# Wider value projections and a split pool of raw weight buffers in a PE-bound mLSTM / HGRN2 trunk

## The chip, the cores and the metric

The kernel runs on one core of one Trainium2 chip. The metric is device time in microseconds (us) of one execution; a version is judged by the median of several. TensorE (PE) multiplies matrices: a stationary operand of 128 x 128 is loaded first (PEld), then a moving operand of up to 512 columns streams through, and results accumulate in PSUM, eight banks of 512 float32 columns per partition. VectorE (DVE) and ScalarE (ACT) do elementwise work, GpSimd (POOL) a little, and SyncE (SP) issues nearly all transfers from memory, in the order of its queue.

## The reference

One layer over 512 tokens of width 1024, in float32. One projection `u = x W_in + b_in` of 14,344 columns feeds two mixers:

- A, mLSTM, four heads of width 512: query and key (causal convolution of four taps, SiLU), value, output gate, and two scalar gates per head. `h = num / max(|den|, exp(-m))`, where `num` is the decayed, causal score matrix times the values and `den` its row sum; then a LayerNorm per head and a sigmoid gate.
- B, HGRN2, eight heads of width 128: forget gate f, key 1 - f, query (SiLU), value ("input" `hi`), output gate; a gated recurrence, a root-mean-square norm and a sigmoid gate.

Then

```
mix = (sigmoid(g_A) * (h_A P_A) + sigmoid(g_B) * (h_B P_B)) W_out
x = LN(alpha x + mix)
x = LN(alpha x + (silu(x W_gate) * (x W_up)) W_down)
```

The kernel computes both recurrences in closed form over the 512 tokens: for mLSTM a 512 x 512 causal weight matrix per head, for HGRN2 a chain of block levels per pair of heads.

## The kernel before, in words

**Float32 products.** Every large product is made from two float32r parts of each operand, `hi` (a rounded copy, ACT) and `lo` (the rest, DVE), as three matmuls: hi hi, hi lo, lo hi (`mm3`, L83 to L86). `split` (L88) makes the two parts.

**Weights.** `fetch` loads a chunk of weights of 512 KB into a raw buffer (`load_w`, L91: pool `rp`, tag `wraw`, five buffers, `WRAW`) and splits it (`split_w`, L96: three buffers each of `whi` and `wlo`). A raw buffer is free again when both halves of the split have read it. A chunk is 24 matmuls of 512 columns, or 48 of 256.

**Two forms of projection.** `proj_sub` (L141) makes 128 features of all 512 tokens: the weights are stationary, x transposed (`xh`, `xl`) moves with 512 columns. `natural_proj` (L156) makes 256 features with tokens on the partitions: x is stationary, the weights move with 256 columns; four row tiles of 128 tokens share two PSUM banks of pool `pp`, and `natural_half` (L149) adds four of the eight k steps from one chunk.

**The stages, in the order of the code.**

1. x is loaded and transposed. The first 256 value columns of head 0 and the scalar gates are projected from a separate load, 264 columns at a time.
2. Four mLSTM heads (loop at L455): eight chunks of key and query features with the score matmuls, the projection onto P_A of the head before (`project_a`), the values (`natural_proj` and `values`, L474 to L477: two calls per head, one for head 0), four chunks of the output gate, with attention (`attend`, L397) and transposes in between. The value tiles `vh`, `vl` have 514 columns: 256 values, two columns of ones (which give `den`), 256 values. Attention makes two products, of 258 and 256 columns.
3. Two chunks of the first merge gate, and the last `project_a`. Then the pool `mp` of the mLSTM stage is closed and the pool `hp` of the HGRN2 stage takes its memory.
4. Four pairs of HGRN2 heads (`h_units`, L527): f, query, values (`natural_proj`, two adds of 512 columns into `v`), output gate: eight chunks per pair. The block levels of a pair (`h_chain`, L711) run while the next pair is projected.
5. Fourteen more chunks of merge gates; `sgb`, in the buffers of f, K, Q and v, keeps the gates of B.
6. Projection onto P_B (L738), eight chunks: DVE multiplies with the gate, adds the A side, and the sum is split into `mxh`, `mxl`.
7. The pools `hp` and `pp` are closed (L744 to L746). Pool `lp` (L750) opens on the side of `rp`, and takes memory that `hp` had: `lng`, `lnb` (LayerNorm rows, L756 and L757), `z` (rows of x, L827), and small tiles. `natural_pass` (L774) multiplies with W_out, two row tiles at a time, in eight chunks of one k step by 1024 columns, each chunk adding to what the first began. LayerNorm, the gate and up projections and the down projection (22 chunks, twice) follow.

**What sets the order.** `defer(n, f)` puts work off until n ticks have passed, and each projected chunk ends with a `tick`: so the small matmuls of attention and of the chain are written between chunks. The tile framework then plans the order on each engine and queue: work that is ready goes first, and among ready work what stands first in the code. It adds the waits. A tile waits for its buffer, and a pool that is opened on memory of a closed pool waits for it.

Of the kernel before, what the change touches and what calls it, by code (L numbers as in the profile page):

```python
# [8 lines left out]
F32 = mybir.dt.float32  # L9
# [20 lines left out]
O_HQ, O_HF, O_HI, O_HG, O_GA, O_GB = 8200, 9224, 10248, 11272, 12296, 13320  # L30
SOFF = [0, 512, 896, 1152]
SCOLS = 1280
WRAW = 5


@with_exitstack
def tile_hybrid_trunk(
# [50 lines left out]
    def split(src, hi, lo):  # L88
        return nc.scalar.copy(hi, src), nc.vector.tensor_sub(lo, src, hi.bitcast(F32))  # L89

    def load_w(src, kk, nn):  # L91
        raw = rp.tile([P, kk, nn], F32, tag="wraw", name="wraw", bufs=WRAW)
        nc.sync.dma_start(raw, src.rearrange("(k p) n -> p k n", p=P))
        return raw

# [7 lines left out]
    def fetch(src, kk, nn):  # L103
        return split_w(load_w(src, kk, nn))
# [4 lines left out]
    def psum(pl, tag, shape=(P, 512), bufs=None):  # L109
        kw = {} if bufs is None else {"bufs": bufs}  # L110
        return pl.tile(list(shape), F32, tag=tag, name=tag, **kw)
# [20 lines left out]
    def tick(w=1.0):  # L132
        for e in pend:
            e[0] -= w
        due = [e for e in pend if e[0] <= 0]
        for e in due:
            pend.remove(e)
        for e in due:
            e[1]()
# [6 lines left out]
                k == 0, k == kk - 1)  # L146
        return ps

    def natural_half(outs, s_, wh, wl, shared=True):  # L149
        for t in range(NT):  # L150
            for k in range(4):
                kx = 4 * s_ + k
                mm3(outs[t], xh[:, kx, t * P:(t + 1) * P], xl[:, kx, t * P:(t + 1) * P], wh[:, k], wl[:, k],
                    kx == 0 and not (shared and t % 2), kx == KD - 1, skip_group_check=True)

    def natural_proj(off):  # L156
        vps = [psum(pp, "pp", (P, 2, 256)) for _ in range(2)]
        outs = [vps[t // 2][:, t % 2] for t in range(NT)]
        for s_ in range(2):
            natural_half(outs, s_, *fetch(win[s_ * 512:(s_ + 1) * 512, off:off + 256], 4, 256))  # L160
            if s_ == 0:
                tick()
        return vps

# [54 lines left out]
        wv.append((hi, lo))  # L219
    vps0 = [psum(*((pp, "pp") if t < 3 else (px, "px")), (P, 264)) for t in range(NT)]  # L220
    for s_ in range(2):
        natural_half(vps0, s_, *wv[s_], shared=False)


    cols = cst.tile([P, 3 * P], F32, name="cols")
# [150 lines left out]
                                           op0=OP.mult, op1=OP.mult)  # L376
            split(w32[:, :n], wth[:, o:o + n], wtl[:, o:o + n])

    def values(h, u2, vps, vt_):
        vh, vl, vb = vt_  # L380
        us2 = slice(u2 * 256, (u2 + 1) * 256)
        vs2 = slice(u2 * 258, u2 * 258 + 256)
        for g in range(2):
            vt = mp.tile([P, 2, 256], F32, tag="w32", name="vt", bufs=4)
            nc.vector.tensor_add(vt, vps[g], vb[:, None, us2].to_broadcast([P, 2, 256]))
            split(vt, vh[:, 2 * g:2 * g + 2, vs2], vl[:, 2 * g:2 * g + 2, vs2])

    def value_tiles(h):
        vh = mp.tile([P, NT, 514], FR, tag="vh", name="vh")
        vl = mp.tile([P, NT, 514], FR, tag="vl", name="vl")  # L390
        nc.vector.memset(vh[:, :, 256:258].bitcast(F32), 1.0)
        nc.vector.memset(vl[:, :, 256:258].bitcast(F32), 0.0)
        vb = mp.tile([P, MD], F32, tag="vb", name="vb")
        nc.sync.dma_start(vb, b_in[:, O_MV + h * MD:O_MV + (h + 1) * MD].to_broadcast([P, MD]))
        return vh, vl, vb

    def attend(h, tiles, wth, wtl, vh, vl, hn):  # L397
        for i in tiles:
            nps = [psum(px, "px", (P, 258)), psum(sp, f"s{i % 3}", (P, 256))]
            for e, vs in enumerate((slice(0, 258), slice(258, 514))):  # L400
                for j in range(i + 1):
                    o = SOFF[j] + (i - j) * P
                    mm3(nps[e], wth[:, o:o + P], wtl[:, o:o + P], vh[:, j, vs], vl[:, j, vs], j == 0, j == i)
            den = nps[0][:, 256:257]
            sm = mp.tile([P, 24], F32, tag="sm", name="sm", bufs=2)
            for e in range(2):
                nc.vector.bn_stats(sm[:, 6 * e:6 * e + 6], nps[e][:, 0:256])
            nc.vector.tensor_scalar(sm[:, 14:15], den, -1.0, em[:, i, h:h + 1], op0=OP.mult, op1=OP.max)
            nc.vector.tensor_tensor(sm[:, 15:16], den, sm[:, 14:15], op=OP.max)
            nc.vector.bn_aggr(sm[:, 12:14], sm[:, 0:12].rearrange("p (a b) -> p a b", a=2))  # L410
            nc.vector.reciprocal(sm[:, 16:17], sm[:, 15:16])
            nc.vector.tensor_mul(sm[:, 17:18], sm[:, 16:17], sm[:, 16:17])
            nc.vector.tensor_scalar(sm[:, 18:19], sm[:, 13:14], sm[:, 17:18], HEAD_EPS, op0=OP.mult, op1=OP.add)
            nc.gpsimd.tensor_tensor(sm[:, 19:20], sm[:, 18:19], nhalf[:, 0:1], op=OP.pow)
            nc.vector.tensor_mul(sm[:, 20:21], sm[:, 19:20], sm[:, 16:17])
            nc.vector.scalar_tensor_tensor(sm[:, 21:22], sm[:, 12:13], -1.0, sm[:, 20:21], op0=OP.mult, op1=OP.mult)
            for e in range(2):
                nc.scalar.activation(hn[:, i, e * 256:(e + 1) * 256], nps[e][:, 0:256], AF.Identity,
                                     bias=sm[:, 21:22], scale=sm[:, 20:21])
# [35 lines left out]
    for h in range(MH):  # L455
        sps = [psum(sp, "s0"), psum(sp, "s1"), psum(sp, "s2")]
        sview = [sps[0][:, 0:512], sps[1][:, 0:384], sps[2][:, 0:256], sps[2][:, 256:384]]
        wth = mp.tile([P, SCOLS], FR, tag="wth", name="wth")
        wtl = mp.tile([P, SCOLS], FR, tag="wtl", name="wtl")
        for c in range(4):  # L460
            kk, qq = [feature_chunk(h, c, w) for w in range(2)]

            def s_step(c=c, kk=kk, qq=qq, sview=sview, wth=wth, wtl=wtl, h=h):
                scores(sview, c, kk, qq)
                if c == 3:
                    weights(h, sview, wth, wtl)

            defer(2, s_step)
            if c == 0 and h == 0:
                gates_1()  # L470
            if c == 1 and h > 0:
                project_a(h - 1, *held)
        vt_ = vt0 if h == 0 else value_tiles(h)
        for u2 in range(1 if h == 0 else 0, 2):  # L474
            vps = natural_proj(O_MV + h * MD + u2 * 256)
            values(h, u2, vps, vt_)
            tick()  # L477
        vh, vl, _ = vt_
        hn = mp.tile([P, NT, MD], F32, tag="hn", name="hn")
        for n in range(2):  # L480
            defer(1 + n, lambda h=h, ts_=(2 * n, 2 * n + 1), a=(wth, wtl, vh, vl, hn): attend(h, ts_, *a))
        ht = bp.tile([P, 2, 4, T], FR, tag="hbh", name="ht")
        hth, htl = ht[:, 0], ht[:, 1]
        for c in range(4):
            off = O_MO + h * MD + c * P
            wh, wl = fetch(in_cols(off), KD, P)
            ps = proj_sub(wh, wl, 0, xh, xl)
            so = mp.tile([P, T], F32, tag="w32", name="so", bufs=4)
            nc.scalar.activation(so, ps, AF.Sigmoid, bias=bcol(off))
            tick()  # L490
            defer(2 if c < 3 else 1, lambda h=h, c=c, a=(so, hn, hth, htl): gate_chunk(h, c, *a))
        held = (hth, htl)
# [29 lines left out]
    for i in range(2):  # L522
        ad = hp_.tile([P, 8, P], F32, name=f"ad{i}")
        nc.gpsimd.memset(ad, 0.0)
        ads.append(ad)

    def h_units(pr):  # L527

        st = dict(pr=pr, ad=ads[pr % 2])
        for name in ("f", "K", "Q", "og"):  # L530
            st[name] = hp_.tile([P, 2, T], F32, tag=name, name=name, bufs=2)
        st["v"] = hp_.tile([P, NT, 256], F32, tag="v", name="v", bufs=2)
        st["tot"] = hp_.tile([P, 1024], F32, tag="tot", name="tot", bufs=1)
        f, K, Q, og, v = (st[k] for k in ("f", "K", "Q", "og", "v"))
        for c in range(2):
            n = 2 * pr + c
            wh, wl = fetch(in_cols(O_HF + n * P), KD, P)
# [6 lines left out]
        for c in range(2):  # L544
# [4 lines left out]
            nc.scalar.activation(sg, ps, AF.Sigmoid, bias=bcol(O_HQ + n * P))  # L549
            nc.vector.scalar_tensor_tensor(Q[:, c], ps, bcol(O_HQ + n * P), sg, op0=OP.add, op1=OP.mult)  # L550
            tick()
        vb = hp_.tile([P, 256], F32, tag="vb", name="vb")
        nc.sync.dma_start(vb, b_in[:, O_HI + pr * 256:O_HI + (pr + 1) * 256].to_broadcast([P, 256]))
        vps = natural_proj(O_HI + pr * 256)
        for g in range(2):
            nc.vector.tensor_add(v[:, 2 * g:2 * g + 2], vps[g], vb[:, None, :].to_broadcast([P, 2, 256]))
        tick()
        for c in range(2):
            n = 2 * pr + c
            wh, wl = fetch(in_cols(O_HG + n * P), KD, P)  # L560
# [118 lines left out]
    def h_out(st, c):  # L679
        n = 2 * st["pr"] + c  # L680
        ad, a1, a2, og = st["ad"], st["a1"], st["a2"], st["og"]
        ops = psum(px, "px", (P, NT, P))
        vc = lambda j: st["v"][:, j, c * P:(c + 1) * P]
        for i in range(NT):
            terms = [(ad[:, 4 * c + i], i)]
            if i % 2 == 1:
# [40 lines left out]
    for n in range(2, KD):  # L727
        sg = hp_.tile([P, T], F32, tag="sg", name="sga", bufs=2)
        merge_gate(O_GA, n, sg)
        nc.vector.tensor_mul(accn(n), accn(n), sg)  # L730
    sgb2 = [hp_.tile([P, 2, T], F32, tag=tag, name="sgb", bufs=2) for tag in ("f", "K", "Q", "v")]
    sgbs = [sgb2[n // 2][:, n % 2] for n in range(KD)]
    for n in range(KD):
        merge_gate(O_GB, n, sgbs[n])
# [13 lines left out]

    pf = pool(ctx, "pf", bufs=8, space=PSUM)
    lp = pool(ctx, "lp", side="right")  # L750
    sum_scale = float(ALPHA)

    def ln_rows(g_d, b_d):
# [162 lines left out]
```

## Time and profile before

| what | value |
|---|---|
| median of 3 runs | 1333.22 us (1332.94 to 1334.21) |
| the profiled execution | 1334.2 us, span from first to last instruction 1332.5 us |
| mean granted TensorE clock | 0.997 |
| busy: PE / DVE / ACT | 1315.9 / 753.9 / 537.0 us |
| mean DMA rate | 106 GB/s |

How to read the rows: a group has line, engine, operation, result <- operands by the program's names, shapes and count, then the busy time of the group, the mean length of one in ns, and the idle time of the engine before them with what ended it. A line of the timeline has start and length in us. A line of the waits has who waited for whom, the sum, how often, and the longest. A line of the windows has the stretch, its length, the busy time (and instructions) of each engine, the granted clock, the share of the DMA engines and GB/s. "SPq" is the queue of SP. Matmuls are pipelined, so their lengths overlap.

### The profile page before, as it was taken

To read this page: it belongs to the slowest core of one execution; us is meant where nothing else is said; L and a number is where in the kernel's file an instruction comes from. 1 tells how busy PE (TensorE), PEld (TensorE's weight loads), DVE (VectorE), ACT (ScalarE), POOL (GpSimd) and SP (SyncE) were. 2 spreads that over 40 slices of the span, in tenths; PEclk is the share of its full clock that TensorE was granted. 3 is DMA by queue.
4 is the path that set the end of the run, shared out by engine and by line. 5 is a ranking of instruction groups with operands and counts; after the bars stand their busy time and mean duration, and the time that the engine had idled before them with its cause. 6 is when DMAs were issued, how large, how long until landed. Compare 5 with 4: busy or idle time off the path is not lost.

```text
span 1332.5 us, 17405 instructions
## 1 busy us (share of the span) xinstructions
PE 1315.9 (99%) x7023; PEld 1136.1 (85%) x7023; DVE 753.9 (57%) x1140; ACT 537.0 (40%) x811; POOL 41.2 (3%) x78
## 2 busy tenths in 40 slices
PE   8999999999999999999999999999999999999997
PEld 7788889888988998889898988887898888888885
DVE  5764656566555755557586754345765433334575
ACT  4773553444342533332424333323773222233332
POOL 0000000000000002000000000000000000000001
PEclk9999999999999999999999999999999999999999
DMA  8222333233323323332232222235664343335672
GB/s 235 80 72 79 88 88 92 75 81 94 88 79 89 86 79 84 98 96 70 63 83 64 71 72 64 79 95 201 197 186 128 95 129 101 102 95 162 192 229 81
DMA packets 189424, 141.31 MB, mean 106 GB/s; under 512 B 5728, under 2 KB 178592, under 8 KB 189344
## 3 DMA queue, kind: packets, MB, share of 16 engines
q1 hardware_dynamic: 188288, 140.17, 37.0%
q8 instruction: 55, 0.90, 0.3%
q14 instruction: 25, 0.20, 0.0%
q10 hardware_dynamic: 1056, 0.03, 0.0%
HBM read 138.09 MB, written 2.10 MB: 105 GB/s over the span
## 4 chain that ended last, share of the span: by engine, by line
PE 97%; DVE 1%; ACT 1%; DMA 1%; issue 0%; POOL 0%; SPq 0%; DVEq 0%; POOLq 0%
PE pp L84 19%; PE pp L85 19%; PE pp L86 19%; PE pf L84 10%; PE pf L85 10%; PE pf L86 10%; PE px L646 2%; PE px L692 1%; PE s L85 1%; PE s L86 1%; PE s L84 1%; PE px L579 1%; DMA xn<-in_x_dram 1%; PE px L424 1%; PE px L663 1%; PE px L84 0%
## 5 line engine op out<-in xcount | busy, mean ns | idle before, releaser
L89 ACT CAST whi<-wraw 128x1024 fp32r<-128x1024 f32 x246 | 258.1, 1050 | 592.3 <-PE pp L85 253.8
L89 DVE TENSOR_TENSOR wlo<-wraw,whi 128x1024 fp32r<-128x1024 f32 x246 | 300.6, 1223 | 272.4 <-ACT whi L89 270.0
L84 PE MATMUL pp<-xh,whi 128*128 128x512 f32 x704 | 278.1, 395 | 0.0
L86 PE MATMUL pp<-xh,wlo 128*128 128x512 f32 x704 | 275.5, 391 | 0.0
L85 PE MATMUL pp<-xl,whi 128*128 128x512 f32 x704 | 275.4, 391 | 0.0
L86 PEld LDWEIGHTS pp<-xh,wlo 128*128 128x128 f32 x704 | 132.6, 188 | 28.3 <-issue 0.4
L84 PEld LDWEIGHTS pp<-xh,whi 128*128 128x128 f32 x704 | 132.7, 188 | 27.6 <-issue 1.0
L85 PEld LDWEIGHTS pp<-xl,whi 128*128 128x128 f32 x704 | 132.6, 188 | 26.2
L86 PE MATMUL pf<-x1h,wlo 128*128 128x512 f32 (+1 forms) x416 | 148.4, 357 | 0.8 <-DVE wlo L89 0.8
L84 PE MATMUL pf<-x1h,whi 128*128 128x512 f32 (+1 forms) x416 | 148.4, 357 | 0.0
L85 PE MATMUL pf<-x1l,whi 128*128 128x512 f32 (+1 forms) x416 | 148.3, 356 | 0.0
L84 PE MATMUL pp<-whi,xh 128*128 128x256 f32 x352 | 100.6, 286 | 0.0
L85 PE MATMUL pp<-wlo,xh 128*128 128x256 f32 x352 | 99.8, 284 | 0.0
L86 PE MATMUL pp<-whi,xl 128*128 128x256 f32 x352 | 99.5, 283 | 0.0
L86 PEld LDWEIGHTS pf<-x1h,wlo 128*128 128x128 f32 x416 | 78.6, 189 | 12.1 <-DVE wlo L89 1.0
L84 PEld LDWEIGHTS pf<-x1h,whi 128*128 128x128 f32 x416 | 78.6, 189 | 11.3
L85 PEld LDWEIGHTS pf<-x1l,whi 128*128 128x128 f32 x416 | 78.6, 189 | 11.3
L357 DVE SCALAR_TENSOR_TENSOR y<-u,cols,y 128x512 f32<-128x512 f32 x96 | 71.9, 750 | 6.1 <-ACT y L355 2.6
L85 PE MATMUL pf<-wlo,g 128*128 128x512 f32 x176 | 68.6, 390 | 0.0
L86 PE MATMUL pf<-whi,g 128*128 128x512 f32 x176 | 68.5, 389 | 0.0
L84 PE MATMUL pf<-whi,g 128*128 128x512 f32 x176 | 68.4, 389 | 0.0
L85 PEld LDWEIGHTS pp<-wlo,xh 128*128 128x128 f32 x352 | 67.5, 192 | 0.1
(251 smaller groups left out, 1940.3 us busy)
## 6 DMA issues: line engine op xcount, KB each, us to landing
wraw<-in_w_in_dram SPq DMA_DIRECT2D x110, 512.0 KB, 3.9
wraw<-in_w_ffn_down_dram SPq DMA_DIRECT2D x44, 512.0 KB, 3.6
wraw<-in_w_ffn_gate_dram SPq DMA_DIRECT2D x26, 512.0 KB, 3.9
wraw<-in_w_ffn_up_dram SPq DMA_DIRECT2D x26, 512.0 KB, 3.9
wraw<-in_w_proj_a_dram SPq DMA_DIRECT2D x16, 512.0 KB, 3.5
wraw<-in_w_out_dram SPq DMA_DIRECT2D x16, 512.0 KB, 3.8
wraw<-in_w_proj_b_dram SPq DMA_DIRECT2D x8, 512.0 KB, 4.3
xn<-in_x_dram SPq DMA_DIRECT2D x4, 512.0 KB, 5.0
```

What stands on the lines that cost most here:

```text
L84: nc.tensor.matmul(ps, lh, rh, start=start, stop=False, **kw)
L85: nc.tensor.matmul(ps, lh, rl, start=False, stop=False, **kw)
L86: nc.tensor.matmul(ps, ll, rh, start=False, stop=stop, **kw)
L89: return nc.scalar.copy(hi, src), nc.vector.tensor_sub(lo, src, hi.bitcast(F32))
L357: nc.vector.scalar_tensor_tensor(y, u[:, tap:tap + T], cwcol(tap, ch), y, op0=OP.mult, op1=OP.add)
L424: nc.tensor.transpose(tps[:, i * P:(i + 1) * P], hn[:, i, c * P:(c + 1) * P], ident)
L579: nc.tensor.matmul(ps.rearrange("p j n -> p (j n)"), ones_r, part.rearrange("p a b -> p (a b)"), start=(i == 0), stop=(i == 1))
L646: nc.tensor.matmul(lps[:, 4 * c + j], K[:, c, js], mov, start=True, stop=True)
L663: nc.tensor.matmul(lps[:, b], K[:, c, b * P:(b + 1) * P], Q[:, c, 256:512], start=True, stop=True)
L692: nc.tensor.matmul(ops[:, i], at, vc(j), start=(e == 0), stop=(e == len(terms) - 1))
```

## The change

- The values of heads 1 to 3 come from one call of a new `natural_wide`: 512 columns at once, four chunks of two k steps by 512 columns, four accumulators of a whole bank each: three of `pp`, one of `px`. It ticks after each of the first three chunks. `values` adds the bias and splits by row tile. Head 0 keeps its one call of `natural_proj`.
- The columns of ones move to the end of `vh` and `vl`; attention's products are of 256 and 258 columns, and `den` comes from the second.
- HGRN2: the values of pairs 0 and 1 are made by one wide call at the start of pair 1, those of pairs 2 and 3 at the start of pair 2. `v` has three buffers instead of two, the bias row is 512 columns wide and lies in a buffer of the tag `sg`. Pairs 0 and 3 have six chunks, pairs 1 and 2 ten.
- `rp` has four raw buffers. All loads are counted; once `lp` is open, every load whose number is a multiple of five goes to one further buffer, `wmore`, in `lp`.

The core of the diff:

```diff
-WRAW = 5
+WRAW = 4
...
+    more, loads = [], [0]
+
     def load_w(src, kk, nn):
-        raw = rp.tile([P, kk, nn], F32, tag="wraw", name="wraw", bufs=WRAW)
+        loads[0] += 1
+        if more and loads[0] % (WRAW + 1) == 0:
+            raw = more[0].tile([P, kk, nn], F32, tag="wmore", name="wraw", bufs=1)
+        else:
+            raw = rp.tile([P, kk, nn], F32, tag="wraw", name="wraw", bufs=WRAW)
         nc.sync.dma_start(raw, src.rearrange("(k p) n -> p k n", p=P))
...
+    def natural_wide(off):
+
+        vps = [psum(*((pp, "pp") if t < 3 else (px, "px"))) for t in range(NT)]
+        for s_ in range(4):
+            natural_part(vps, 2 * s_, *fetch(win[s_ * 256:(s_ + 1) * 256, off:off + 512], 2, 512))
+            if s_ < 3:
+                tick()
+        return vps
...
+            for t in range(NT):
+                vt = mp.tile([P, MD], F32, tag="w32", name="vt", bufs=4)
+                nc.vector.tensor_add(vt, vps[t], vb)
+                split(vt, vh[:, t, 0:512], vl[:, t, 0:512])
...
-            nps = [psum(px, "px", (P, 258)), psum(sp, f"s{i % 3}", (P, 256))]
-            for e, vs in enumerate((slice(0, 258), slice(258, 514))):
+            nps = [psum(px, "px", (P, 256)), psum(sp, f"s{i % 3}", (P, 258))]
+            for e, vs in enumerate((slice(0, 256), slice(256, 514))):
...
-        for u2 in range(1 if h == 0 else 0, 2):
-            vps = natural_proj(O_MV + h * MD + u2 * 256)
-            values(h, u2, vps, vt_)
-            tick()
+        values(natural_proj(O_MV + 256) if h == 0 else natural_wide(O_MV + h * MD), vt_)
+        tick()
...
+        if pr in (1, 2):
+            lo = 0 if pr == 1 else 2
+            vb = hp_.tile([P, 512], F32, tag="sg", name="vb", bufs=2)
+            nc.sync.dma_start(vb, b_in[:, O_HI + lo * 256:O_HI + (lo + 2) * 256].to_broadcast([P, 512]))
+            vps = natural_wide(O_HI + lo * 256)
+            for q in range(2):
+                vs_[lo + q] = hp_.tile([P, NT, 256], F32, tag="v", name="v", bufs=3)
+            for t in range(NT):
+                for q in range(2):
+                    qs = slice(q * 256, (q + 1) * 256)
+                    nc.vector.tensor_add(vs_[lo + q][:, t], vps[t][:, qs], vb[:, qs])
+            tick()
...
     lp = pool(ctx, "lp", side="right")
+    more.append(lp)
```

`natural_part` is `natural_half` with the first k step and the number of k steps as parameters.

More of the change, by code (lines that the diff above doesn't have):

```diff
@@ L147, in proj_sub, with natural_part @@
         return ps
-    def natural_half(outs, s_, wh, wl, shared=True):
+    def natural_part(outs, k0, wh, wl, shared=False):
         for t in range(NT):
-            for k in range(4):
-                kx = 4 * s_ + k
+            for k in range(wh.shape[1]):
+                kx = k0 + k
                 mm3(outs[t], xh[:, kx, t * P:(t + 1) * P], xl[:, kx, t * P:(t + 1) * P], wh[:, k], wl[:, k],
@@ L159, in natural_proj @@
         for s_ in range(2):
-            natural_half(outs, s_, *fetch(win[s_ * 512:(s_ + 1) * 512, off:off + 256], 4, 256))
+            natural_part(outs, 4 * s_, *fetch(win[s_ * 512:(s_ + 1) * 512, off:off + 256], 4, 256), shared=True)
             if s_ == 0:
+                tick()
[5 more added lines that the diff above has]
+            if s_ < 3:
                 tick()
@@ L221, in tile_hybrid_trunk @@
     for s_ in range(2):
-        natural_half(vps0, s_, *wv[s_], shared=False)
+        natural_part(vps0, 4 * s_, *wv[s_])
     cols = cst.tile([P, 3 * P], F32, name="cols")
@@ L377, in weights, with values @@
             split(w32[:, :n], wth[:, o:o + n], wtl[:, o:o + n])
-    def values(h, u2, vps, vt_):
+    def values(vps, vt_):
         vh, vl, vb = vt_
[L381 to L386, printed above, removed]
+        if len(vps) == 2:
+            for g in range(2):
+                vt = mp.tile([P, 2, 256], F32, tag="w32", name="vt", bufs=4)
+                nc.vector.tensor_add(vt, vps[g], vb[:, None, 256:512].to_broadcast([P, 2, 256]))
+                split(vt, vh[:, 2 * g:2 * g + 2, 256:512], vl[:, 2 * g:2 * g + 2, 256:512])
+        else:
+            for t in range(NT):
+                vt = mp.tile([P, MD], F32, tag="w32", name="vt", bufs=4)
+                nc.vector.tensor_add(vt, vps[t], vb)
+                split(vt, vh[:, t, 0:512], vl[:, t, 0:512])
     def value_tiles(h):
@@ L390, in value_tiles @@
         vl = mp.tile([P, NT, 514], FR, tag="vl", name="vl")
-        nc.vector.memset(vh[:, :, 256:258].bitcast(F32), 1.0)
-        nc.vector.memset(vl[:, :, 256:258].bitcast(F32), 0.0)
+        nc.vector.memset(vh[:, :, 512:514].bitcast(F32), 1.0)
+        nc.vector.memset(vl[:, :, 512:514].bitcast(F32), 0.0)
         vb = mp.tile([P, MD], F32, tag="vb", name="vb")
@@ L403, in attend @@
                     mm3(nps[e], wth[:, o:o + P], wtl[:, o:o + P], vh[:, j, vs], vl[:, j, vs], j == 0, j == i)
-            den = nps[0][:, 256:257]
+            den = nps[1][:, 256:257]
             sm = mp.tile([P, 24], F32, tag="sm", name="sm", bufs=2)
@@ L525, in tile_hybrid_trunk @@
         ads.append(ad)
+    vs_ = {}
     def h_units(pr):
@@ L531, in h_units @@
             st[name] = hp_.tile([P, 2, T], F32, tag=name, name=name, bufs=2)
-        st["v"] = hp_.tile([P, NT, 256], F32, tag="v", name="v", bufs=2)
         st["tot"] = hp_.tile([P, 1024], F32, tag="tot", name="tot", bufs=1)
-        f, K, Q, og, v = (st[k] for k in ("f", "K", "Q", "og", "v"))
+        f, K, Q, og = (st[k] for k in ("f", "K", "Q", "og"))
+        if pr in (1, 2):
[10 more added lines that the diff above has]
+            tick()
         for c in range(2):
@@ L551, in h_units @@
             tick()
[L552 to L557, printed above, removed]
         for c in range(2):
@@ L682, in h_out @@
         ops = psum(px, "px", (P, NT, P))
-        vc = lambda j: st["v"][:, j, c * P:(c + 1) * P]
+        vc = lambda j: vs_[st["pr"]][:, j, c * P:(c + 1) * P]
         for i in range(NT):
@@ L730, in tile_hybrid_trunk @@
         nc.vector.tensor_mul(accn(n), accn(n), sg)
-    sgb2 = [hp_.tile([P, 2, T], F32, tag=tag, name="sgb", bufs=2) for tag in ("f", "K", "Q", "v")]
+    sgb2 = [hp_.tile([P, 2, T], F32, tag=tag, name="sgb", bufs=n_) for tag, n_ in (("f", 2), ("K", 2), ("Q", 2), ("v", 3))]
     sgbs = [sgb2[n // 2][:, n % 2] for n in range(KD)]
```

## The prediction

> **What bounds the kernel now.** I read the page first: busy times, the chain that ended last, groups, DMA issues.
>
> ```profile
> span 1332.5 us, 17405 instructions
> ...
> PE 1315.9 (99%) x7023; PEld 1136.1 (85%) x7023; DVE 753.9 (57%) x1140; ACT 537.0 (40%) x811; POOL 41.2 (3%) x78
> ...
> PE 97%; DVE 1%; ACT 1%; DMA 1%; issue 0%; POOL 0%; SPq 0%; DVEq 0%; POOLq 0%
> ...
> L84 PE MATMUL pp<-whi,xh 128*128 128x256 f32 x352 | 100.6, 286 | 0.0
> ...
> wraw<-in_w_in_dram SPq DMA_DIRECT2D x110, 512.0 KB, 3.9
> ...
> wraw<-in_w_proj_a_dram SPq DMA_DIRECT2D x16, 512.0 KB, 3.5
> ...
> wraw<-in_w_proj_b_dram SPq DMA_DIRECT2D x8, 512.0 KB, 4.3
> ```
>
> TensorE (PE) is the bound. The stage windows (length, then busy time of PE, PEld, DVE, ACT, POOL, granted clock, DMA share, GB/s) say where it has slack:
>
> ```profile
> 80.00:540.00 460.00, 460.00 (x2541) 402.63 (x2540) 274.52 (x488) 193.51 (x280) 16.67 (x33) 1.00 0.31 86
> 540.00:860.00 320.00, 320.00 (x1874) 281.03 (x1873) 194.51 (x280) 113.19 (x221) 8.09 (x8) 1.00 0.28 75
> 860.00:913.00 53.00, 53.00 (x234) 43.56 (x233) 25.04 (x31) 15.15 (x20) 0.00 (x0) 1.00 0.33 98
> 913.00:1324.00 411.00, 409.36 (x2001) 346.63 (x2000) 206.25 (x247) 161.71 (x213) 4.92 (x7) 1.00 0.49 148
> ```
>
> None, from 80 to 913 us. So time can be won there only by cheaper matmuls, and any wait of PE is added in full. Matmuls overlap, so the mean of 286 ns isn't what one costs; that is the distance between starts. The timeline of PE, inside a head's value projection (256 columns) and inside the down projection (512 columns, also with activations stationary and weights moving):
>
> ```profile
> 204.82 0.28 PE L84 MATMUL pp<-whi,xh 128*128 128x256 f32 x1
> ...
> 209.74 0.28 PE L86 MATMUL pp<-whi,xl 128*128 128x256 f32 x1
> ```
>
> ```profile
> 1250.05 0.39 PE L86 MATMUL pf<-whi,g 128*128 128x512 f32 x1
> ...
> 1254.36 0.39 PE L84 MATMUL pf<-whi,g 128*128 128x512 f32 x1
> ```
>
> There are 41 steps between the first two, 4.92 / 41 = 0.1200 us, and 19 between the others, 4.31 / 19 = 0.2268 us.
>
> **The wider projections: -6.3 us.** The three lines of mm3 have 3 x 352 = 1056 matmuls of 256 columns: 11 calls of 96. Head 0 keeps one call. The ten others (six for heads 1 to 3, four for HGRN2) had 960; five wide calls have 4 parts x 4 row tiles x 2 k x 3 = 96 of 512 columns each, 480. The difference is 480 x (2 x 0.1200 - 0.2268) = 6.3 us, all on the path. Weight loads and splits stay four of 512 KB per 512 columns.
>
> The Trainium skill's page "TensorE: Matmul & The Clock Gate", section "Back-to-back issue gap", gives N/2.4 + 2.5 ns, so it would make this 480 x 2.5 ns = 1.2 us (an estimate from that page) and the forecast 5.1 us later. The rows above show some 13 ns beside the columns and decide.
>
> **Evacuations and order: 0.** In heads 1 to 3 the four adds and splits remain, now by row tile and all behind the last part. In that part a row tile takes 6 matmuls, so the first bank is complete 18 x 0.2268 = 4.1 us before PE wants it again. For HGRN2 an add becomes two halves, eight per wide call, each bounded above by the 512-column add:
>
> ```profile
> L556 DVE TENSOR_TENSOR v<-pp,vb x8: 682/692/693, 571.3 to 754.0; 128x512 f32<-128x512 f32 x8
> ```
>
> Two of them take at most 1.4 us, inside the 4.1. If DVE were late by more, the next chunk would wait, at most 2 us per wide call. The fourth bank comes from px, which its other users (transposes, attention) leave free in these stretches. In attention the ones column goes to the second product: 258 columns change places with 256. The count of ticks per mLSTM head is unchanged; in HGRN2 pairs 1 and 2 have ten, pairs 0 and 3 six, so pair 2's chain ends beside the first merge gates. DVE is busy 194.5 of 320 us there. I take 0 for all this, with 0 to 2 us as bounds.
>
> **Four buffers instead of five, up to the end of projection B: 0.** The waits of the SP queue and of the engines:
>
> ```profile
> SPq L93 <- DVE wlo L89: 1039.3, 217, 14.8
> ...
> SPq L553 <- DVE v L556: 14.5, 3, 5.6
> ...
> SPq L756 <- DVE mxl L89: 0.3, 1, 0.3
> ```
>
> ```profile
> ACT whi L89 <- PE pp L85: 253.8, 78, 7.4
> ```
>
> Loads wait for a free buffer, and the casts for PE to release a split pair, not for data. One buffer fewer issues a load one chunk later, 24 x 0.2268 = 5.4 us. The first load of w_out goes out at 877.56 (below) for a matmul at 913.90, 36 us ahead, and lands in about 4. The HGRN2 bias load, now in an sg buffer behind sigmoid and square tiles, can hold the loads behind it on SP for a chunk or two, as it held them 5.6 us at the worst; the same lead covers that.
>
> **The first load of w_out: the term that decides.** Line by line the loads before w_out are 110 + 16 + 8 = 134, and remain so. The counter counts all of them, and once the lp pool exists every fifth load goes to its single wmore buffer. The first load of w_out is number 135: it goes there. When may a tile of lp be written? The SP queue and then all engines at that place:
>
> ```profile
> 877.56 38.41 SPq L93 DMA_DIRECT2D wraw<-in_w_out_dram  x8
> 916.30 0.33 SPq L756 DMA_DIRECT2D lng<-in_ln_g_dram  x1
> 916.68 0.42 SPq L757 DMA_DIRECT2D lnb<-in_ln_b_dram  x1
> 917.16 0.99 SPq L827 DMA_DIRECT2D z<-in_x_dram  x2
> 919.29 0.33 SPq L93 DMA_DIRECT2D wraw<-in_w_out_dram  x1
> ```
>
> ```profile
> 912.64 0.39 PE L86 MATMUL pp<-hbh,wlo 128*128 128x512 f32 x1
> ...
> 913.06 0.69 DVE L741 TENSOR_TENSOR sgb<-pp,sgb 128x512 f32<-128x512 f32 x1 [2.29 <-PE pp L86]
> ...
> 913.90 0.47 PE L84 MATMUL pf<-whi,mxh 128*128 128x512 f32 x1 [0.88 <-DVE sgb L741]
> ...
> 915.53 0.69 DVE L89 TENSOR_TENSOR mxl<-sgb,mxh 128x512 fp32r<-128x512 f32 x1
> ```
>
> lng is the first tile of lp. Its load waits for the last mxl (the row of 0.3 us above), an operation that touches neither lng nor lp: it is the last reader of hp, the pool whose memory lp takes over. The queue's order agrees: eight w_out loads that stand behind lng in the code went ahead of it. So lp opens when all of hp is done, at 916.22, 2.3 us after PE has begun w_out. Until now that harmed nothing, because w_out's chunks came through rp. After the change chunk 0 can't be asked for earlier, and every product of w_out accumulates onto chunk 0's, so PE can't take chunks 1 to 4 first. Nothing else is left for it: no deferred work is pending there.
>
> What its load costs, from the DMA issues (median to landing) of the window 917 to 921 and of the window 877 to 916:
>
> ```profile
> z<-in_x_dram SPq DMA_DIRECT2D x2, 512.0 KB, 8.6
> ...
> wraw<-in_w_out_dram SPq DMA_DIRECT2D x1, 512.0 KB, 8.2
> ```
>
> ```profile
> wraw<-in_w_out_dram SPq DMA_DIRECT2D x8, 512.0 KB, 3.6
> ```
>
> In the code lng, lnb and the two z come ahead of chunk 0, and all five become possible at the same moment, so I put it fifth, issued 918.2, as the load of 919.29 was fifth, and use that load's 8.2 us, not the 3.6 of a load alone. Landing at 926.4. Then the cast and the subtraction, as the chunk after shows them:
>
> ```profile
> 916.95 1.05 ACT L89 CAST whi<-wraw 128x1024 fp32r<-128x1024 f32 x1 [1.82 <-PE pf L86]
> ```
>
> ```profile
> 918.03 1.23 DVE L89 TENSOR_TENSOR wlo<-wraw,whi 128x1024 fp32r<-128x1024 f32 x1 [1.82 <-ACT whi L89]
> ```
>
> 926.4 + 0.1 + 1.05 + 1.23 = 928.8. One product may run before wlo, so the stream restarts in effect at 928.6 instead of 913.9: **+14.7 us** (all clock readings here before subtracting the 6.3). With the load alone at 3.6 us in fifth place it is 10.1; I take the upper value because the four transfers ahead are the same. Chunks 1 to 4 lie in rp by then and cost 1.23 us each on DVE against 12 x 0.2268 = 2.7 on PE: no second stall.
>
> **The clock after the stall: +2.2 us.** The windows around a stretch of four-column matmuls:
>
> ```profile
> 41.00:43.20 2.20, 2.20 (x22) 2.16 (x20) 2.17 (x4) 2.16 (x3) 0.00 (x0) 1.00 0.13 23
> 43.30:46.70 3.40, 3.40 (x10) 2.62 (x11) 3.40 (x7) 1.68 (x3) 0.00 (x0) 0.52 0.40 133
> 46.70:50.00 3.30, 3.30 (x16) 2.70 (x15) 2.40 (x4) 0.28 (x1) 0.00 (x0) 0.97 0.63 159
> ```
>
> After little array work the granted clock was half for 3.4 us, which loses 1.7 us. An idle stretch of 15 us should do the same; between none and two such windows it is 0 to 3.4, and I take a little over one. The Trainium skill, same page, section "Part 1: The HAM clock gate (the "warmup" mystery)", says the clock halves after about 3.4 us of idle and returns after a busy window of that length; the row of 0.52 agrees.
>
> **The sum.** -6.3 + 14.7 + 2.2 = +10.6. The profiled execution took 1334.2 us beside its span of 1332.5, so it would take 1344.8. It lies 1.0 above the median shown, 1333.2, so I predict 1343.8 for a median.
>
> **The rivals.**
> (1) Chunk 0's load goes out ahead of the four others. For it: it is as ready as they are, and nothing but the planner's choice puts it last. Against: between 916 and 919 the queue follows the code. Issued 916.3, landed 919.9, PE restarts 922.1: 8.2 - 6.3 + 2.2 = +4.1, 1337.3.
> (2) The other side: wmore isn't held, because its own addresses are free early (the chain's temporaries end long before). Then PE never waits and 1333.2 - 6.3 = 1326.9. It decides if the load lands by about 905, ahead of its cast and subtraction. Against it: lng was held by an operation of another tile.
> (3) On top of the forecast the main stage stalls: the bias load, a late bank or pair 2's displaced chain, 2 us at each of five wide calls and no more: +10, 1353. Against it: 36 us of lead.
>
> **How the numbers follow.** Forecast 0.66, rival 1 0.12, rival 2 0.12, rival 3 0.10. The forecast's own range: stall 10.1 to 15.1, clock 0 to 3.4, main stage 0 to 2: 1337 to 1347.5. With rival 1 and the low part of rival 3 it is 1336 to 1348, which leaves out rival 2 and some of rival 3. About 0.2% (2.7 us) is what a measurement of this kernel can tell from no change: faster is rival 2, 0.11; slower 0.85; within, 0.04, for a stall that happens to be as small as the gain.
>
> **What would show it.** Right: 512-column steps of 0.227 us in the value stages and the first w_out matmul near 907.6 + 14.7 = 922; an idle row of PE before it of some 14 us released by DVE wlo or ACT whi; among the SP rows four w_out loads, then lng, lnb, z, z and a fifth weight load; a granted clock near 0.5 behind it. Wrong: w_out's loads all ahead of lng, PE idle there about 1 us as now, or PE idle in the windows between 80 and 900.

## The result and the profile after

The changed kernel is slower: 1341.9 us (1341.65 to 1343.69, five runs) against 1333.31 (1332.94 to 1334.56, five runs). The ratio is 1.0064, with a 95% interval of 1.0052 to 1.0076: 8.6 us more, where 10.6 were forecast. The profiled execution took 1343.69 us.

From the page of the changed kernel: span, busy times, the slices of PE, of the granted clock and of the DMA engines, and the DMA issues that count the loads before w_out.

```profile
span 1341.7 us, 16441 instructions
...
PE 1312.3 (98%) x6543; PEld 1112.1 (83%) x6543; DVE 752.8 (56%) x1148; ACT 536.8 (40%) x811; POOL 43.1 (3%) x78
...
PE   8999999999999999999999999995999999999997
...
PEclk9999999999999999999999999997999999999999
...
wraw<-in_w_in_dram SPq DMA_DIRECT2D x110, 512.0 KB, 3.9
...
wraw<-in_w_proj_a_dram SPq DMA_DIRECT2D x16, 512.0 KB, 3.4
...
wraw<-in_w_proj_b_dram SPq DMA_DIRECT2D x8, 512.0 KB, 4.1
```

There are 480 matmuls fewer (7023 to 6543), and one slice in which PE has a hole and the clock a dip. The loads before w_out are again 110 + 16 + 8 = 134. The waits of PE name the hole (before, its longest single wait outside the start was 0.9 us, for sgb):

```profile
PE pf L84 <- ACT whi L89: 13.5, 1, 13.5
...
PE pf L86 <- DVE wlo L89: 0.8, 1, 0.8
```

The SP queue at that place, then the timelines of DVE, ACT and PE:

```profile
877.29 16.65 SPq L99 DMA_DIRECT2D wraw<-in_w_out_dram  x4
910.23 0.33 SPq L783 DMA_DIRECT2D lng<-in_ln_g_dram  x1
910.61 0.43 SPq L784 DMA_DIRECT2D lnb<-in_ln_b_dram  x1
911.09 0.90 SPq L854 DMA_DIRECT2D z<-in_x_dram  x2
912.03 16.66 SPq L99 DMA_DIRECT2D wraw<-in_w_out_dram  x5
```

```profile
909.46 0.69 DVE L89 TENSOR_TENSOR mxl<-sgb,mxh 128x512 fp32r<-128x512 f32 x1 [0.68 <-ACT mxh L89]
```

```profile
919.71 2.94 ACT L89 CAST whi<-wraw 128x1024 fp32r<-128x1024 f32 x3 [10.28 <-DMA wraw<-in_w_out_dram]
```

```profile
906.93 0.39 PE L86 MATMUL pp<-hbh,wlo 128*128 128x512 f32 x1
...
920.80 1.22 PE L84 MATMUL pf<-whi,mxh 128*128 128x512 f32 x2 [13.49 <-ACT whi L89]
922.06 0.80 PE L85 MATMUL pf<-wlo,mxh 128*128 128x512 f32 x1
```

Four loads of w_out (numbers 136 to 139, chunks 1 to 4) go out during projection B. Then the queue stands until the last mxl ends at 910.15; this wait of 16.2 us (0.3 before) is the line of SP's waits:

```profile
SPq L783 <- DVE mxl L89: 16.2, 1, 16.2
```

lng, lnb, z, z follow, and only then chunk 0, issued 912.03 and cast from 919.71. The casts are three in a row: chunks 1 and 2 had lain in their buffers for long. PE begins w_out at 920.80.

The stages of the two profiles, in us between the same instructions:

| from, to | before | after | difference |
|---|---|---|---|
| first instruction to head 0's first 256-column matmul | 81.14 | 81.61 | +0.47 |
| to the last matmul of projection B | 831.50 | 825.32 | -6.18 |
| to the first matmul of w_out | 1.26 | 13.87 | +12.61 |
| to the first matmul of the gate projection | 45.42 | 47.64 | +2.22 |
| to the last instruction | 373.15 | 373.27 | +0.12 |
| span | 1332.47 | 1341.71 | +9.24 |

The wide projections gave what was forecast, and one wait with its aftermath cost more than twice as much. The second row is the gain. A wide value stage in the new trace has 26 steps between these two rows, 5.90 / 26 = 0.2269 us, the fourth bank (px) no slower than the others:

```profile
325.07 0.39 PE L84 MATMUL pp<-whi,xh 128*128 128x512 f32 x1
...
330.97 0.39 PE L86 MATMUL pp<-whi,xl 128*128 128x512 f32 x1
```

The windows (PE, PEld, DVE, ACT, POOL, granted clock, DMA share, GB/s) show that no new idle time came in the stages that the change rebuilt, and the clock around the wait:

```profile
80.00:540.00 460.00, 460.00 (x2269) 390.90 (x2268) 275.85 (x490) 194.99 (x282) 16.67 (x33) 1.00 0.31 86
540.00:860.00 320.00, 320.00 (x1692) 272.25 (x1692) 193.82 (x287) 113.64 (x222) 9.93 (x8) 1.00 0.28 76
...
921.00:925.00 4.00, 3.96 (x9) 2.69 (x10) 3.28 (x3) 1.65 (x2) 0.00 (x0) 0.50 0.43 130
925.00:930.00 5.00, 5.00 (x23) 4.12 (x23) 1.40 (x2) 2.09 (x2) 0.00 (x0) 1.00 0.71 233
```

PE restarts at half clock and is back at full clock at 925: 9 matmuls in 4 us, 23 in the next 5. The first nine steps of w_out take 4.33 us (920.80 to 925.13), where they took 2.13 before: that is the whole fourth row. Not all of it is the clock. Two hi hi products go first, and the weight load of the third waits for wlo:

```profile
922.06 0.29 PEld L85 LDWEIGHTS pf<-wlo,mxh 128*128 128x128 f32 x1 [0.76 <-DVE wlo L89]
```

The first three steps take 1.85 us, where three of the 0.43 us that the later ones take at half clock make 1.3. So some 0.5 us is the wait for wlo and some 1.7 us the clock (an estimate from these starts).

### The profile page after: what moved, and what is told of

Read it like the earlier page. It is cut to its first block, busy times and chain, and to the rows that moved or that the text cites. A ratio compares the mean times of both kernels' runs of the same rounds, so it can differ in the third digit from the quotient of the medians.

```text
span 1341.7 us, 16441 instructions
## 1 busy us (share of the span) xinstructions
PE 1312.3 (98%) x6543; PEld 1112.1 (83%) x6543; DVE 752.8 (56%) x1148; ACT 536.8 (40%) x811; POOL 43.1 (3%) x78
## 4 chain that ended last, share of the span: by engine, by line
PE 96%; DVE 1%; DMA 1%; ACT 1%; issue 0%; SPq 0%; POOL 0%; DVEq 0%; POOLq 0%; ACTq 0%
PE pp L84 18%; PE pp L86 18%; PE pp L85 18%; PE pf L84 10%; PE pf L85 10%; PE pf L86 10%; PE px L672 2%; PE px L718 1%; PE px L86 1%; PE px L85 1%; PE px L84 1%; PE s L86 1%; PE s L85 1%; PE s L84 1%; PE px L605 1%; DMA wraw<-in_w_out_dram 1%
## 5 line engine op out<-in xcount | busy, mean ns | idle before, releaser
L84 PE MATMUL pp<-whi,xh 128*128 128x512 f32 (+1 forms) x152 | 56.1, 369 | 0.0
L85 PE MATMUL pp<-wlo,xh 128*128 128x512 f32 (+1 forms) x152 | 55.9, 368 | 0.0
L86 PE MATMUL pp<-whi,xl 128*128 128x512 f32 (+1 forms) x152 | 55.8, 367 | 0.0
L84 PE MATMUL pp<-ht,whi 128*128 128x512 f32 x128 | 50.1, 391 | 0.0
```

What stands on the lines that cost most here:

```text
L84: nc.tensor.matmul(ps, lh, rh, start=start, stop=False, **kw)
L85: nc.tensor.matmul(ps, lh, rl, start=False, stop=False, **kw)
L86: nc.tensor.matmul(ps, ll, rh, start=False, stop=stop, **kw)
```

## The experiments

The theory: w_out's chunk 0 is load 135, goes to a buffer of lp, and lp opens only when hp is done. The rivals: that something else in the change costs the time (four raw buffers, displaced work in HGRN2, the wide projections themselves), or that the stall has another cause than lp's opening (the queue alone). The runs came in two groups of four, each with the kernel before on the same chip: 1333.71 us beside the first three and the one with four buffers throughout, 1334.44 beside the others.

**The extra buffer later.**

```diff
-        if more and loads[0] % (WRAW + 1) == 0:
+        if more and loads[0] > 140 and loads[0] % (WRAW + 1) == 0:
```

> The changed kernel, but the extra buffer in lp is used only from load 141 on, so w_out's chunk 0 (load 135) comes through the four buffers that are there already. Theory (lp is held until hp is done, chunk 0 waits for that, and nothing else in the change costs time): the idle time of PE before w_out falls back to about 1 us, no half clock there, 1333.3 - 6.2 = 1327.1 us. Rival (four buffers starve the stages before, or the wide projections gain nothing, and the extra buffer matters little): 1335 us or more, with PE idle elsewhere.

Measured: 1328.56 us, ratio 0.9958 (0.9940 to 0.9976). The waits of PE at w_out are those of the kernel before:

```profile
PE pf L84 <- DVE sgb L767: 0.9, 1, 0.9
PE pf L86 <- DVE wlo L89: 0.8, 1, 0.8
```

With chunk 0 in an old buffer the stall is gone and the gain is left. (The median lies 1.5 above the 1327.1 expected; 0.4 of it is the chip, and the interval, 1325.7 to 1330.5 us, takes the rest in.) Its profile has 825.32 us in the second row of the table, as the changed kernel, and 1.27 in the third.

**Chunk 0's load first in the queue.** In the code, z's loads and the LayerNorm rows stand behind the pass:

```diff
-    g1, b1 = ln_rows(ln1_g, ln1_b)
     for ts_ in ((0, 1), (2, 3)):
-        zs = {}
-        for t in ts_:
...
         pss = natural_pass(w_out[0], KD, lambda k, t: mxh[:, k, t * P:(t + 1) * P],
...
+        zs = {}
+        for t in ts_:
...
+        if ts_[0] == 0:
+            g1, b1 = ln_rows(ln1_g, ln1_b)
```

> The changed kernel with the code of the LayerNorm rows (lng, lnb) and of z moved behind the first pass's loads, so that chunk 0's load is the first transfer when lp opens. Theory (two parts of the stall: lp opens late, and four transfers of 512 KB stand ahead): only the second part goes. Chunk 0 asked for at 910.2, landing after 3.6 us instead of 1.8 + 7.6, PE starts w_out near 914.9 instead of 920.8, the half clock stays: 1341.9 - 5.9 = 1336.0 us. Rival (the stall is the queue alone): about 1328 us. Rival (the place in the queue does nothing): 1341.9 us.

Measured: 1338.72 us, ratio 1.0035 (1.0023 to 1.0047). The SP queue, then the waits of SP and of PE:

```profile
875.59 33.26 SPq L99 DMA_DIRECT2D wraw<-in_w_out_dram  x5
908.90 0.90 SPq L855 DMA_DIRECT2D z<-in_x_dram  x2
```

```profile
SPq L99 <- DVE mxl L89: 16.2, 1, 16.2
```

```profile
PE pf L84 <- ACT whi L89: 7.8, 1, 7.8
```

The fifth of these weight loads is chunk 0's, issued 908.52, right behind the end of the last mxl (908.44), for which it now waits itself, as lng did. The wait of PE fell from 13.5 to 7.8 us, by 5.7 where 5.9 were expected. So both parts are real: about 6 us are the place behind four transfers of 512 KB, and 7.8 remain (0.9 in the kernel before) with chunk 0 already first. The median lies 2.7 above the 1336.0 expected; 0.4 of it is the chip (the kernel before was at 1333.71 there), 1.0 the clock, which in the profile stayed half for 6 us behind the restart instead of 4 (restart to gate projection 48.60 us against 47.64). The rest is not explained.

**The buffers alone.** The kernel before with four raw buffers and the extra one in lp, as in the change's diff, and none of its projections.

> The kernel before with the buffers of the change alone: four raw buffers, and the fifth in lp by the same count; no wide projections. Theory: the same stall without the gain, 1333.3 + 12.6 (longer wait) + 2.2 (half clock and start) = 1348.1 us. Rival (the wide projections themselves move the stage boundary and cause the stall): about 1333 us.

Measured: 1350.44 us, ratio 1.0117 (1.0094 to 1.0139), four executions, 1347.92 to 1353.28. The timeline of PE:

```profile
912.91 0.39 PE L86 MATMUL pp<-hbh,wlo 128*128 128x512 f32 x1
926.82 1.22 PE L84 MATMUL pf<-whi,mxh 128*128 128x512 f32 x2 [13.53 <-ACT whi L89]
```

The same wait, 13.91 us from start to start, without a single wide projection: it is the buffer's. In the profile the span grew by 15.3 us (1347.8 against 1332.5), where 14.8 were expected; the median lies 2.3 above the 1348.1 expected, with only four executions that lie up to 5.4 us apart.

**Four buffers throughout, none in lp.**

```diff
-        if more and loads[0] % (WRAW + 1) == 0:
+        if False:
```

> The changed kernel with four raw buffers throughout, without the extra one. Theory: as the run with the later extra buffer before the w_out stage, 1327.1 us, if four buffers carry the stages that take a chunk every 2.7 us as well (a load is now issued 11.3 us before its cast there and would be 8.6, against 3.6 to land). Rival (five are needed there): PE idle rows in the gate, up and down projections, over 1330 us.

Measured: 1328.79 us, ratio 0.9959 (0.9942 to 0.9975), and the PE waits at w_out of the first experiment. The extra buffer, for which all this was paid, is worth nothing: four are enough also where PE takes a chunk every 2.7 us. This version and the first beat both kernels, and this one is the simpler.

**Four buffers in the kernel before.** `WRAW = 4`, nothing else.

> The kernel before with four raw buffers instead of five and nothing else. Theory: loads are early enough everywhere, 1333.3 us, no change. Rival (the fifth buffer carries the w_out and down stages): slower, PE idle rows released by wlo or whi behind 913 us.

Measured: 1334.55 us, ratio 1.0005 (0.9996 to 1.0015): no difference. The prediction's 0 for this term stands.

**The wide projections one at a time**, with four buffers and none in lp: first heads 1 to 3 alone, then HGRN2 alone.

> Wide value projections of heads 1 to 3 alone; HGRN2 as before; four raw buffers, no extra one. Theory (a pair of 256-column matmuls costs 13.2 ns more than one of 512): 288 x 13.2 ns = 3.8 us less than the kernel before, 1329.5 us. Rival (the gain comes from elsewhere, such as one chunk's place or fewer waits): not in this proportion.

> Wide input projections of HGRN2 alone, with their new places in the pairs; the mLSTM heads as before; four raw buffers, no extra one. Theory: 192 x 13.2 ns = 2.5 us less than the kernel before, 1330.8 us, and the displaced chain of pair 2 costs nothing. Rival (the displaced chain or the bias load in an sg buffer stalls PE): less gain or none, with PE idle between 540 and 860 us.

Measured: 1330.72 us, ratio 0.9979 (0.9967 to 0.9990), and 1332.45 us, ratio 0.9991 (0.9981 to 1.0002), the second not distinguishable from no change by the medians. The profiles are sharper. PE's first 256-column matmul of head 0 and the last of projection B, of the mLSTM run and of the HGRN2 run:

```profile
81.34 0.28 PE L84 MATMUL pp<-whi,xh 128*128 128x256 f32 x1
...
909.09 0.39 PE L86 MATMUL pp<-hbh,wlo 128*128 128x512 f32 x1
```

```profile
85.06 0.28 PE L84 MATMUL pp<-whi,xh 128*128 128x256 f32 x1
...
914.22 0.39 PE L86 MATMUL pp<-hbh,wlo 128*128 128x512 f32 x1
```

827.75 and 829.16 us, against 831.50 before: -3.75 and -2.34, where 288 and 192 pairs at 13.2 ns make 3.8 and 2.5. Together -6.09, beside -6.18 with both. The displaced chain and the bias row in an sg buffer cost at most a tenth or two of a microsecond.

**The extra buffer for chunk 4 instead of chunk 0.**

```diff
-        if more and loads[0] % (WRAW + 1) == 0:
+        if more and loads[0] % (WRAW + 1) == 4:
```

> The changed kernel with the extra buffer used by every fifth load from one place earlier in the count, so that w_out's chunk 4 (load 139) is the first to go through it, and chunks 0 to 3 are not. Theory: chunk 4 lands where chunk 0 landed, near 919.7, its first product can run at 920.8, and PE, which begins w_out near 908.1, needs it 4 x 2.72 us later at 919.0: a wait of 1.8 us, too short for the half clock, so about 2 us above the version without the stall: 1330 us. Rival (any use of lp at this place costs the same, through the queue or through the order of the splits): 1341 us. Rival (a wait of that size suffices for the half clock): 1332 us with a clock record of 0.5 there.

Measured: 1333.63 us, ratio 0.9996 (0.9982 to 1.0009). Waits and windows:

```profile
PE pf L84 <- ACT whi L89: 3.6, 1, 3.6
```

```profile
914.00:918.80 4.80, 4.80 (x23) 3.83 (x21) 0.00 (x0) 0.00 (x0) 0.00 (x0) 1.00 0.95 358
918.80:921.00 2.20, 0.23 (x2) 0.00 (x0) 0.00 (x0) 0.00 (x0) 0.00 (x0) 1.00 1.02 417
921.00:922.60 1.60, 0.00 (x0) 0.00 (x0) 0.01 (x1) 1.09 (x2) 0.00 (x0) 0.53 0.25 100
922.60:928.00 5.40, 5.39 (x13) 4.23 (x14) 3.48 (x3) 1.85 (x2) 0.00 (x0) 0.51 0.55 157
```

PE works through chunks 0 to 3 while the transfers run, so most of the stall is hidden; that part of the expectation held. The size did not: 3.6 us of waiting instead of 1.8, since the cast of chunk 4 began at 921.51 and not near 919.7. Here one more w_out load, issued 909.65, was still under way when lp opened at 910.22. That this is the cause was not tested by itself, but four runs agree with it. Counted from the issue of lng, the fifth of the five loads was cast 9.5 us later in the changed kernel and with the buffers alone, where no other load was under way; with one more under way it was cast 11.2 us later here, and landed 11.2 us later in the kernel before. And the clock did halve, as the second rival had it, though behind a longer wait than it assumed: 13 matmuls in 5.4 us. Wait and clock together cost the whole gain of the projections: from the first product of w_out to the gate projection it took 51.8 us instead of 45.42.

## Why the prediction was right, point by point

**The gain.** Forecast 6.3 us, measured 6.18, and in two parts, 3.75 and 2.34, close to 288 to 192. The distance between starts, not the mean duration, was the right price. The 2.5 ns that the Trainium skill (page "TensorE: Matmul & The Clock Gate", section "Back-to-back issue gap") gives per matmul, for the gap of an isolated one, would have made it 1.2 us; that isn't what these float32r matmuls show.

**Evacuations, order, four buffers.** All put at 0, and all 0 within what the runs resolve. Rival 3, stalls in the main stage, did not come: PE is busy for 460.00 of 460 us and 320.00 of 320.

**Load 135 and the opening of lp.** Right, and shown by taking the buffer away (the stall goes), by putting it in alone (the stall comes) and by putting it at another chunk (the stall moves). Rival 2 rested on the addresses of wmore alone, and is refuted: in the run with chunk 0 first, its load, a tile of lp like lng, waited 16.2 us for the same mxl. Whether lp waits for all of hp or these tiles happened to lie where mxl's operands had been, the runs do not separate. Rival 1 was the place in the queue: the planner kept the order of the code, and the run in which chunk 0 goes first gives its wait, 5.7 us shorter.

**The length of the stall.** Forecast 14.7 us, measured 12.61 for the wait: this is the term that was mis-sized, in three places. Counted from the last matmul of projection B, chunk 0's load went out 5.1 us later (912.03) and not 5.5: no subtraction of wlo stood ahead of the last mxl. The cast began 7.7 us after the issue, not 8.3 (8.2 and the 0.1 to the cast): in the kernel before, the load that gave the price ran beside one more w_out load. And the products began 1.1 us behind the start of the cast, where the forecast, which let one product run before wlo, has 2.1 in effect: two hi hi products went ahead at half clock, and the 0.5 us that was still waited for wlo lies in the fourth row.

**The clock.** Forecast 2.2, measured some 1.7; the wait for wlo fills the fourth row up to 2.22. The forecast took a little over one window of half clock. In fact it was half for 13.6 us, and only 4.2 of them fell on matmuls: that the size came near was in part luck.

**The sum.** +9.24 in the profiles where the forecast had +10.6. Of this 0.47 arose in the first 81 us and is scatter: the run with the extra buffer later has the changed kernel's code there, and took 79.82 us where the changed kernel took 81.61. Without it the distance is 1.8 us.

**The range** of 1336 to 1348 held the time; the likeliest case was the one that came.

## What to carry to other kernels

Before a buffer is moved to another pool, ask when that pool's memory is free, and which transfer will be the first to use it: lp, which opened on the memory of hp, waited in every run for hp's last reader, whichever of its tiles was loaded first, and a prefetch that crosses such a boundary must not depend on it. Where PE has no slack, as here, a single late load costs its whole delay and the half clock behind it, so a gain of 13 ns per matmul pair, however well counted, has to be set against the one step that stops the stream. Count the loads: a condition on a counter is a schedule, and here it decided that the very first chunk behind the boundary, and not a later one, met the pool that was not yet free.

## What the runs showed of the hardware that was not expected

An idle stretch of only 3.6 us was enough for the half clock, and it began some 2 us into that stretch (the rows 918.80 to 922.60 above), earlier than the 3.4 us of idle that the prediction names. It then lasted 6.8 us, of which 5.3 fell on matmuls. The length of the penalty isn't fixed by the length of the idle time: behind a wait of 13.5 us it was 4 us of work, behind one of 7.8 us 6 us. In these two runs, the changed kernel and the one with chunk 0 first, the half clock lasted from 911.4 to 925.0 and from 909.4 to 919.6, wait included:

```profile
911.40:924.90 13.50, 4.06 (x9) 2.79 (x10) 3.50 (x3) 2.94 (x3) 0.00 (x0) 0.50 0.66 231
```

```profile
909.40:919.50 10.10, 6.05 (x13) 4.30 (x14) 3.50 (x3) 3.11 (x4) 0.00 (x0) 0.50 0.90 312
```

So it lasted 6.8, 10.2 and 13.6 us in the three runs: two, three and four times 3.4. In these runs it came in whole steps of that length, and what it cost depended on how much of the last steps fell on work. The Trainium skill, same page, section "Part 1: The HAM clock gate (the "warmup" mystery)", says that the gate looks at windows of 3.4 us that run freely, whatever the kernel does: the three lengths, and the start in the middle of the stretch, agree with that.

The half clock is also a part of the scatter between executions. In the profile of the HGRN2 run the stretch behind the small matmuls of the gates ran at half clock for 6.8 us, where the run without the extra buffer had the full clock over the same stretch; the rows of the one and of the other:

```profile
62.00:68.80 6.80, 6.80 (x17) 4.88 (x16) 2.81 (x5) 6.74 (x12) 2.45 (x6) 0.50 0.28 77
```

```profile
62.00:68.80 6.80, 6.80 (x29) 5.08 (x29) 2.81 (x5) 6.74 (x12) 2.45 (x6) 1.00 0.29 80
```

17 matmuls instead of 29 in the same time: head 0's values start at 85.06 instead of 81.54. PE counts as busy throughout in both. Of the ten profiles this one had 6.8 us of half clock there, the kernel before with four buffers 3.4 us, and the others none. A difference of 3.5 us between two single executions can be this alone, and the stages behind it are better compared between the same two instructions than by the whole time.
